# Gate tiles of the merge moved to the start, in pairs by seven half products, and one merge stage at the end

## The chip, the cores and the metric

The kernel runs on one core of a Trainium2 chip. The metric is the device time of one execution in microseconds (us), as the median of three runs; one further execution was profiled. TensorE (PE in the rows) multiplies, VectorE (DVE), ScalarE (ACT) and GpSimd (POOL) do the elementwise work, and SyncE (SP) issues the transfers.

## The reference

One layer of an encoder for 1024 prompt tokens and 64 sample tokens that share the weights, all in fp32. Four token mixers (A: mLSTM, B: forgetting attention, C: HGRN2, D: convolution and RG-LRU) read columns of one projection of x and give y_m with 512 columns. Each is expanded to 1024 columns and gated by a product of x, and the four are summed:

```python
proj = jnp.einsum('btd,dp->btp', x, w_in) + b_in          # split among the mixers A, B, C, D
...
for m_idx, y_b in enumerate((y_ml, y_fx, y_hg, y_rg)):
    gate = jax.nn.sigmoid(jnp.einsum('btd,de->bte', x, w_mg[m_idx]) + b_mg[m_idx])
    terms.append(gate * jnp.einsum('btw,wd->btd', y_b, w_br[m_idx]))
mix = terms[0] + terms[1] + terms[2] + terms[3]
x1 = layer_norm(DN_ALPHA * x + jnp.einsum('btd,de->bte', mix, w_out), ln1_g, ln1_b)
gate_pre = jnp.einsum('btd,df->btf', x1, w_ff_gate)
up = jnp.einsum('btd,df->btf', x1, w_ff_up)
...
ffn = jnp.einsum('btf,fd->btd', jax.nn.gelu(gate_c) * up, w_ff_down)
x2 = layer_norm(DN_ALPHA * x1 + ffn, ln2_g, ln2_b)
```

The outputs are x2 for both groups and the mixers' states. Only the order and the arithmetic of the gates and of the sum over mixers are touched by the change.

## The kernel before

Activations stand transposed: 128 channels on the partitions, 1088 tokens in three chunks of 384, 384 and 320 columns. Each fp32 operand is split into a high and a low part, and every product is three matmuls (high by high, high by low, low by high; `mm3`, lines 296 to 298). A **dense tile** (`dense`) is 128 output channels of a product of x: for each chunk 8 k-blocks by 3 matmuls into a PSUM buffer of the pool "psd", then one eviction. The pools "psd" and "psm" have two buffers each.

Weights come in the order of a list, `plan`; a tile of 512 KB is loaded by SP two places ahead (`wissue`), its high part converted by POOL (projections, line 259) or ACT (all others, line 261) and its low part by DVE (line 262).

The mixers run in the order D, C, B, A, in units: P_x(u) is the projections of unit u and M_x(u) its recurrence or attention, made of many small matmuls and elementwise operations. `weave` sends the steps of M_x(u-1) and of P_x(u) by turns. The last M of a branch is woven with 12 chunk steps of **gate tiles** (`gates`: a dense tile of x by w_mg, and a tanh on ACT, line 682, into `th`). Then `merge(m, it)` follows: it computes the other four gate tiles, loads y of the branch (`yr`), splits it (lines 701, 702), multiplies by w_br into "psm" (12 matmuls a chunk), and DVE gates the product (line 717: (th + 1) times the product). The sum over branches goes through DRAM: from the second branch on `prev` is loaded from mx_d and added (line 719), and the first three branches store `th` to mx_d.

After the last merge come w_out and the first LayerNorm (F), the FFN's gate and up products (G), and the down projection (H). In G two tiles of 128 outputs are computed together by `pair` (products at line 368): the first two token chunks and the two halves of k form a 2 by 2 block product with seven block products instead of eight, on sums of weight blocks (`wsums`, lines 284 and 285 for the split) and of x blocks (`xsums`); the third chunk is computed plainly. One block product is 12 matmuls of 384 columns.

At the start the nine tiles of x are transposed by PE and split (lines 177 to 189), the projections' biases are transposed, the first tile of P_D(0) runs between these, and `gate_rows` computes 48 small rows (the scalar gates of A and B) from w16r, a gather of 16 columns of w_in (lines 540 to 549).

Of the kernel before, what the change touches and what calls it, by code (L numbers as in the profile page):

```python
# [2 lines left out]

# [16 lines left out]
P = 128  # L20
# [9 lines left out]
NSLOT = 19  # L30
TGRP = ((0, 1, 2), (3, 4, 5), (8, 6, 7))
# [37 lines left out]
def trunk_kernel(ctx: ExitStack, tc: tile.TileContext, I, O, dbg=None):  # L69
# [36 lines left out]
    slot_pool(NSLOT)  # L106
# [33 lines left out]
    maskU = const([P, P], "maskU")  # L140
# [4 lines left out]
    trif = slot([P, P], F32, "trif")  # L145
# [20 lines left out]
    def xtiles(s):  # L166
        for c, (n0, n) in enumerate(CH):
# [32 lines left out]
    def plan_cons(m):  # L200
        for kind, e in (("mg", 0), ("mg", 1), ("mg", 2), ("mg", 3), ("mg", 4), ("mg", 5), ("br", 0), ("br", 2),
                        ("mg", 6), ("mg", 7), ("br", 4), ("br", 6)):
            wide = P if kind == "mg" else 2 * P
            plan.append(((kind, m, e), I["w_" + kind][0, m, :, e * P:e * P + wide].rearrange(
                "(k p) c -> p k c", p=P), 1024 // wide))

    for u in range(4):
        for c0 in (RG_X, RG_G):
            plan.append((("in", c0 + u * P), win(c0 + u * P), 8))
    plan_cons(3)  # L210
    for u in range(4):
# [17 lines left out]
    pairs = {}  # L229
# [92 lines left out]
    def xsums():  # L322


        for j in (0, 1, 3):
            xs[j] = tuple(wide["x"].tile([P, 4, 384], F32R, tag=f"x{j}{i}", name=nm("xs"), bufs=1) for i in range(2))
        xs[2] = tuple(t[1][:, 0:4, :] for t in (xh, xl))
# [12 lines left out]
        for k in range(4):  # L340
            b11, b12, b22 = temp("xf", 0, k), temp("xf", 1, k), temp("xf", 1, k + 4)
            t3.append(temp("x3"))
            V.tensor_tensor(b11, b12, b11, OP.subtract)
            V.tensor_tensor(t3[k], b22, b12, OP.subtract)
            V.tensor_tensor(b22, b22, b11, OP.subtract)
            parts(0, k, b11)
            parts(1, k, b22)
        for k in range(4):
# [3 lines left out]
            parts(2, k, t3[k])  # L352
# [79 lines left out]
    pkr = slot([P, P], F32, "pkr")  # L432
    pk2 = const([P, PK2], "pk2")
    pk2r = slot([P, P], F32, "pk2r")
    xt = {}

    def xload(*tts):
        for tt in tts:
            xt[tt] = slot([P, D], F32, "xt")
# [1343 lines left out]
```

## Time and profile before

| what | value |
|---|---|
| median of three runs | 2143.22 us (2140.59 to 2143.59) |
| the profiled execution | 2141.45 us |
| its span, first to last instruction | 2139.7 us |
| mean granted clock of TensorE | 0.998 |
| PE busy | 2101.1 us, 98% of the span |
| DVE busy | 1151.5 us, 54% |
| ACT busy | 737.1 us, 34% |
| POOL busy | 223.7 us, 10% |

The engines work side by side; a share is that of the whole span, and stages with different limits lie in it. Matmuls are pipelined, so the time printed beside one is longer than the distance from its start to the next one's.

### The profile page before, as it was taken

The numbers are of one execution on the slowest core, as the hardware profiler recorded it, in microseconds if no ns is written. First come the engines' busy times: TensorE is split into PE (matmuls) and PEld (weight loads), VectorE is DVE, ScalarE is ACT, GpSimd is POOL, SyncE is SP. The second block draws the span as 40 slices with busy tenths as digits, with TensorE's granted clock in tenths as the row PEclk, the third lists the DMA queues.
The fourth block names the chain that finished last, engine by engine and source line by source line (L and its number), as shares of the span: only waits on it lengthen the run. The fifth ranks groups of instructions, "written<-read, shape, count | busy, mean of one in ns | idle before, by whom it ended". The sixth has DMA issues, their size and how long they took to land.

```text
span 2139.7 us, 31840 instructions
## 1 busy us (share of the span) xinstructions
PE 2101.1 (98%) x13035; PEld 1955.5 (91%) x13035; DVE 1151.5 (54%) x2202; ACT 737.1 (34%) x1277; POOL 223.7 (10%) x232
## 2 busy tenths in 40 slices
PE   8999999999999999999999999999999999999998
PEld 7999999888899988889999989899889999998886
DVE  4643245665543466555332144546459766666655
ACT  3664114555321234344310123324134333334341
POOL 1100011220100322200001101000120000000112
PEclk9999999999999999999999999999999999999999
DMA  5112321111143222321432212135211222227652
GB/s 153 53 61 71 103 75 40 44 45 33 52 148 132 82 81 61 92 82 41 131 136 82 63 38 65 43 123 194 80 74 51 80 88 74 79 87 282 224 198 100
DMA packets 193229, 200.29 MB, mean 94 GB/s; under 512 B 14588, under 2 KB 165448, under 8 KB 193084
## 3 DMA queue, kind: packets, MB, share of 16 engines
q1 hardware_dynamic: 193084, 198.26, 28.8%
q8 instruction: 102, 1.67, 0.3%
q14 instruction: 43, 0.35, 0.1%
HBM read 154.80 MB, written 43.43 MB: 93 GB/s over the span
## 4 chain that ended last, share of the span: by engine, by line
PE 51%; DVE 2%; DMA 1%; ACT 0%; issue 0%; POOL 0%; SPq 0%; DVEq 0%; ACTq 0%
PE pss L368 8%; PE psd L296 7%; PE psd L298 7%; PE psd L297 7%; PE pss L1693 5%; PE psd L1693 2%; PE psm L1693 2%; PE psm L297 2%; PE psm L296 2%; PE psm L298 2%; PE pss L296 1%; PE pss L297 1%; PE pss L298 1%; PE psm L368 1%; PE psm L1330 1%; PE psm L1117 0%
## 5 line engine op out<-in xcount | busy, mean ns | idle before, releaser
L296 PE MATMUL psd<-xh,wh 128*128 128x384 f32 (+1 forms) x1920 | 643.2, 335 | 0.9 <-ACT xh L178 0.9
L298 PE MATMUL psd<-xh,wl 128*128 128x384 f32 (+1 forms) x1920 | 631.4, 329 | 0.0
L297 PE MATMUL psd<-xl,wh 128*128 128x384 f32 (+1 forms) x1920 | 630.1, 328 | 0.8 <-DVE xl L179 0.8
L262 DVE TENSOR_TENSOR wl<-wr,wh 128x1024 fp32r<-128x1024 f32 x179 | 222.7, 1248 | 327.6 <-ACT wh L261 202.5
L296 PEld LDWEIGHTS psd<-xh,wh 128*128 128x128 f32 x1920 | 362.9, 189 | 7.9 <-issue 3.0
L297 PEld LDWEIGHTS psd<-xl,wh 128*128 128x128 f32 x1920 | 361.6, 188 | 1.8 <-DVE xl L179 1.0
L298 PEld LDWEIGHTS psd<-xh,wl 128*128 128x128 f32 x1920 | 361.6, 188 | 0.4
L261 ACT ACTIVATE wh<-wr 128x1024 fp32r<-128x1024 f32 x131 | 139.0, 1061 | 376.6 <-PE psd L297 127.5
L297 PE MATMUL psm<-yl,wh 128*128 128x384 f32 (+1 forms) x384 | 125.9, 328 | 1.4 <-DVE yl L702 1.4
L298 PE MATMUL psm<-yh,wl 128*128 128x384 f32 (+1 forms) x384 | 125.7, 327 | 0.0
L296 PE MATMUL psm<-yh,wh 128*128 128x384 f32 (+1 forms) x384 | 125.0, 328 | 0.6 <-ACT yh L701 0.6
L259 POOL TENSOR_SCALAR wh<-wr 128x1024 fp32r<-128x1024 f32 x48 | 52.7, 1098 | 669.7 <-PE psd L297 266.5
L682 ACT ACTIVATE th<-psd,bhalf 128x384 f32<-128x384 f32 (+1 forms) x96 | 53.4, 558 | 156.0 <-PE psd L298 156.0
L717 DVE SCALAR_TENSOR_TENSOR th<-th,psm 128x384 f32<-128x384 f32 (+1 forms) x96 | 50.9, 531 | 104.5 <-PE psm L298 103.2
L296 PE MATMUL psd<-x1h,wh 128*128 128x320 f32 (+1 forms) x272 | 85.2, 313 | 0.6 <-DVE x1l L189 0.6
L298 PE MATMUL psd<-x1h,wl 128*128 128x320 f32 (+1 forms) x272 | 84.9, 312 | 0.0
L297 PE MATMUL psd<-x1l,wh 128*128 128x320 f32 (+1 forms) x272 | 84.7, 312 | 0.0
L1496 POOL TENSOR_TENSOR lrs<-lrs,mhalf 128x1 f32<-128x1 f32 (+1 forms) x16 | 9.8, 614 | 665.9 <-ACT hh L1640 423.9
L1180 DVE CUSTOM_DVE_ANT_0 Pt<-pss,fcb 128x128 f32<-128x128 f32 (+7 forms) x64 | 48.2, 752 | 57.6 <-PE pss L1175 57.1
L297 PEld LDWEIGHTS psm<-yl,wh 128*128 128x128 f32 x384 | 72.1, 188 | 2.1 <-DVE yl L702 2.1
L296 PEld LDWEIGHTS psm<-yh,wh 128*128 128x128 f32 x384 | 71.8, 188 | 1.5 <-ACT yh L701 1.2
L298 PEld LDWEIGHTS psm<-yh,wl 128*128 128x128 f32 x384 | 72.1, 188 | 0.0
(536 smaller groups left out, 3907.4 us busy)
## 6 DMA issues: line engine op xcount, KB each, us to landing
wr<-in_w_in_dram SPq DMA_DIRECT2D x48, 512.0 KB
wr<-in_w_ff_down_dram SPq DMA_DIRECT2D x48, 512.0 KB
wr<-in_w_mg_dram SPq DMA_DIRECT2D x32, 512.0 KB
mx_d<-th SPq DMA_DIRECT2D x24, 544.0 KB
prev<-mx_d SPq DMA_DIRECT2D x24, 544.0 KB
wr<-in_w_br_dram SPq DMA_DIRECT2D x16, 512.0 KB
wr<-in_w_ff_gate_dram SPq DMA_DIRECT2D x16, 512.0 KB
wr<-in_w_ff_up_dram SPq DMA_DIRECT2D x16, 512.0 KB
```

The costliest lines, as they stand in the source:

```text
L259: G.tensor_scalar(h, raw, 1.0, 1.0, OP.mult, OP.mult)
L261: S.activation(h, raw, AF.Copy)
L262: V.tensor_sub(l, raw, h.bitcast(F32))
L296: PE.matmul(ps, wh, mh, start=i == 0, stop=False)
L297: PE.matmul(ps, wh, ml, start=False, stop=False)
L298: PE.matmul(ps, wl, mh, start=False, stop=i == n - 1)
L368: PE.matmul(ps, w[:, k, :], x[:, k, :], start=start and k == 0 and i == 0, stop=k == 3 and i == 2, skip_group_check=not start)
L682: S.activation(th[:, n0:n0 + n], ps, AF.Tanh, bias=b, scale=0.5)
L717: V.scalar_tensor_tensor(th[:, n0:n0 + n], th[:, n0:n0 + n], 1.0, ps[:, :n], OP.add, OP.mult)
L1180: V.tensor_tensor_reduce(Pt[:, 0:L].rearrange("p (b n) -> p b n", b=nb), ps.rearrange("p (b n) -> p b n", b=2)[:, 0:nb, 0:n], cbs[hh][:, 0 ...
L1330: PE.matmul(ps[0:w, 0:w], kt[r, t0:t0 + w], qt[r, t0:t0 + w], start=True, stop=True)
L1693: PE.matmul(ps[hf], a[:, f % 8, o:o + P], w[:, 0, sl], start=f == 0 and i == 0, stop=f == 15 and i == (2 if tt < 8 else 1))
```

## The change

The 32 gate tiles no longer depend on where the mixers are, since they need x alone. Thirty of them now come first: four of branch 3 plainly while x is still being transposed, then 13 pairs through `pair`, with the sums of x made by `xsums(False)` into tiles of their own. Every `th` is stored to DRAM (`th_d`), 544 KB each. The last two, (0,6) and (0,7), run plainly under M_A(1). The mixers follow one another without a merge: the last M of a branch is woven with the next branch's projections, M_C(3) with 7 of the steps of P_B(0), and M_A(1) with 14 steps, of which six are the last two gate tiles and eight are merge pieces (one chunk of one output tile) of branch 3. Then all other merges follow. y is loaded from y_d and split into the tiles of x, which x no longer needs (`ysplit`), `th` is loaded from th_d, and the sum over branches stays in eight tiles on chip (`res`), chunk by chunk. The load order `plan` follows. At the start the first weights are gate tiles, so ACT converts them, and the gates' biases (pk2r) are loaded ahead of the projections' biases (pkb).

In numbers of instructions: PE has 11475 instead of 11631 rows, DVE 2377 instead of 2142, ACT 75 more, and SP issues 32 stores and 32 loads of `th` where it issued 24 stores and 24 loads of the running sum.


```diff
+PLAIN = ((3, 0), (3, 2), (0, 6))
...
+    th_d = [[dp.tile([P, T], F32, name=f"th_d{m}_{e}") for e in range(8)] for m in range(4)]
+
+    def gates(m, es):
+        for e in es:
+            th = slot([P, T], F32, "th")
+            b = bhalf[:, m * 8 + e:m * 8 + e + 1]
+
+            def ev(c, n0, n, ps, th=th, b=b):
+                S.activation(th[:, n0:n0 + n], ps, AF.Tanh, bias=b, scale=0.5)
+                if c == 2:
+                    SP.dma_start(th_d[m][e], th)
+            yield from dense(("mg", m, e), ev)
+
+    def gate_pair(m, e):
+        ths = [slot([P, T], F32, "th") for _ in range(2)]
+        bs = [bhalf[:, m * 8 + e + i:m * 8 + e + i + 1] for i in range(2)]
+
+        def act(i, n0, n, src):
+            S.activation(ths[i][:, n0:n0 + n], src, AF.Tanh, bias=bs[i], scale=0.5)
+
+        def add(i, n0, ps, other):
+            V.tensor_tensor(ths[i][:, n0:n0 + 384], ps, other, OP.add)
+            if n0 == 384:
+                a = 384 * i
+                act(i, a, 768 - a, ths[i][:, a:768])
+                if i == 0:
+                    SP.dma_start(th_d[m][e], ths[0])
+
+        def put(i, n0, n, ps):
+            act(i, n0, n, ps)
+            if i == 1 and n0 == 0:
+                SP.dma_start(th_d[m][e + 1], ths[1])
+        yield from pair(("mg", m, e), ("mg", m, e + 1), add, put)
+
+    g0, g1 = gates(3, (0,)), gates(3, (1,))
+    for c in range(3):
+        for tt in range(3 * c, 3 * c + 3):
+            if c:
+                xsplit(xt[tt], tt, tt != 3 * c + 1)
+        next(g0)
+        next(g1)
+    run(g0, g1, gates(3, (2, 3)))
+    xsums(False)
...
+    def ysplit(m, c):
+
+        n0, n = CH[c]
+        for q in range(0, 4, 2):
+            r = slot([P, 2, 384], s="yr")
+            for i in range(2):
+                SP.dma_start(r[:, i, 0:n], y_d[m][q + i][:, n0:n0 + n])
+            k = 4 * (m % 2) + q
+            h = xh[c][:, k:k + 2, :]
+            S.activation(h, r[:, :, 0:n], AF.Copy)
+            V.tensor_sub(xl[c][:, k:k + 2, :], r[:, :, 0:n], h.bitcast(F32))
...
+    def merge(m, es, rows=None):
+
+        for e in es:
             wh, wl = wget(("br", m, e))
             for g in range(2):
...
+                th = slot([P, T], F32, "th")
+                SP.dma_start(th, th_d[m][e + g])
+                if m == 3:
+                    res.append(th)
                 for c, (n0, n) in enumerate(CH):
...
+                    ps = bank("m")[:, :n]
+                    y = [[t[c][:, 4 * (m % 2) + k, :] for k in range(4)] for t in (xh, xl)] if rows is None else \
+                        [[t[k][:, n0:n0 + n] for k in range(4)] for t in rows]
+                    mm3(ps, [(wh[:, k, g * P:(g + 1) * P], wl[:, k, g * P:(g + 1) * P], y[0][k], y[1][k])
+                             for k in range(4)])
+                    sl = slice(n0, n0 + n)
+                    V.scalar_tensor_tensor(th[:, sl], th[:, sl], 1.0, ps, OP.add, OP.mult)
+                    if m < 3:
+                        V.tensor_tensor(res[e + g][:, sl], res[e + g][:, sl], th[:, sl], OP.add)
+                    yield
...
-    def branch(m, Pg, Mg, n, nP, nM, it, ng=4):
-        for u in range(1, n):
-            weave(Mg(u - 1), nM, Pg(u), nP)
-        weave(Mg(n - 1), nM, gates(m, range(4)), 12)
-
-    first = P_D(0)
-    for c in range(1, 3):
-        next(first)
-        for tt in range(3 * c, 3 * c + 3):
-            xsplit(xt[tt], tt, tt != 3 * c + 1)
-        next(first)
-    next(first)
+    def until_flushed(g):
+
+        while tails:
+            next(g)
+            flush()
+        run(g)
+
+    for m, e in mgs:
+        if (m, e) not in PLAIN:
+            run(gate_pair(m, e))
+    slot_pool(NSLOT)
+    phase("D")
     gate_rows()
-    run(first)
-    branch(3, P_D, M_D, 4, 6, 10, 0)
-    merge(3, 0)
+    run(P_D(0))
+    weave(M_D(0), 10, P_D(1), 6)
+    weave(chain(M_D(1), fox_rows()), 13, P_D(2), 6)
+    weave(M_D(2), 10, P_D(3), 6)
+    weave(chain(M_D(3), ml_rows()), 17, P_C(0), 12)
     out_D()
     phase("C")
-    weave(chain(fox_rows(), ml_rows()), 10, P_C(0), 12)
-    branch(2, P_C, M_C, 4, 12, 19, 1)
-    merge(2, 1)
+    for u in range(1, 4):
+        weave(M_C(u - 1), 19, P_C(u), 12)
+    g = P_B(0)
+    weave(M_C(3), 19, islice(g, 7), 7)
+    until_flushed(g)
     phase("B")
-    run(P_B(0))
-    branch(1, P_B, M_B, 4, 9, 23, 2)
-    merge(1, 2)
+    for u in range(1, 4):
+        weave(M_B(u - 1), 23, P_B(u), 9)
+    weave(M_B(3), 23, P_A(0), 18)
     phase("A")
-    run(P_A(0))
-    branch(0, P_A, M_A, 2, 18, 21, 3)
-    res = merge(0, 3)
+    weave(M_A(0), 21, P_A(1), 18)
+
+    def last_gates():
+        for i, _ in enumerate(gates(0, (6, 7))):
+            if i >= 3:
+                xtiles("y", (i - 3,))
+                ysplit(3, i - 3)
+            yield
+
+    g = chain(last_gates(), merge(3, (0, 2)))
+    weave(M_A(1), 21, islice(g, 14), 14)
+    until_flushed(g)
+    for c in range(3):
+        ysplit(2, c)
+    run(merge(3, (4, 6)))
+    for c in range(3):
+        ysplit(1, c)
+    run(merge(2, (0, 2, 4, 6)))
+    rows = yrows()
+    run(merge(1, (0, 2, 4, 6)), merge(0, (0, 2, 4, 6), rows))
```

Where instructions now stand (order of issue on one engine; the names are tiles of the program with running numbers, written `out<-in`).

SP's queue, before, in the start: the load of w16r behind two loads of projection weights.

```order
L251 DMA wr_312<-in_w_in_dram 128x8x128
L251 DMA wr_380<-in_w_in_dram 128x8x128
L540 DMA w16r_527<-in_w_in_dram 128x8x8
L541 DMA w16r_527<-in_w_in_dram 128x8x8
L543 DMA b_55_530<-in_b_in_dram 8x1
```

SP's queue, after, where the pairs end and branch D begins; th_2847 to th_3029 are gates of the last two pairs.

```order
L516 DMA th_d_2_228<-th_2847 128x1088
L263 DMA wr_3331<-in_w_in_dram 128x8x128
L521 DMA th_d_5_231<-th_3029 128x1088
L263 DMA wr_3503<-in_w_in_dram 128x8x128
L516 DMA th_d_4_230<-th_3028 128x1088
L601 DMA w16r_3205<-in_w_in_dram 128x8x8
L602 DMA w16r_3205<-in_w_in_dram 128x8x8
L604 DMA b_374_3208<-in_b_in_dram 8x1
```

w16r now stands behind the stores of the gates; on PE, 37 matmuls of the first projections stand between the last product of the last pair and the 48-row products that read it.

PE, before, where M_C(3) begins: 24 matmuls into psd_5072 stand between the first and the second of these rows of transposes.

```order
L957 MATMUL psm_5059<-ident,vT_4538 128x128 x4
L296 MATMUL psd_5072<-xh_118,wh_4738 128x384
...
L957 MATMUL psm_5098<-ident,vT_4538 128x128 x4
L957 MATMUL psm_5104<-ident,vT_4538 64x128
L296 MATMUL psd_5107<-xh_120,wh_4738 128x384
...
L957 MATMUL psm_5133<-ident,kU_5055 128x128 x4
```

PE, after, at the same place (xh is a chunk of x, wh_6494 a projection weight of branch B): 13 matmuls into psd stand between the second and the last group of v transposes.

```order
L1012 MATMUL psm_6789<-ident,vT_6294 128x128 x4
L1012 MATMUL psm_6795<-ident,vT_6294 128x128 x4
L310 MATMUL psd_6801<-xh_131,wl_6298 128x320
L308 MATMUL psd_6857<-xh_127,wh_6494 128x384
...
L1012 MATMUL psm_6827<-ident,vT_6294 64x128
L308 MATMUL psd_6857<-xh_127,wh_6494 128x384
...
L1012 MATMUL psm_6830<-ident,kU_6785 128x128 x4
L1012 MATMUL psm_6836<-ident,kU_6785 128x128 x4
```

The transposes and what follows from them stand closer together.

DVE, before, in M_A(1): a step of the unit, with the low part of one weight (L262) among its operations.

```order
L1340 TENSOR_SCALAR kp_12617<-psm_12612,aw_12348 128x64
L1339 TENSOR_TENSOR we_12622<-we_12622,psm_12615 128x128
L262 TENSOR_TENSOR wl_12694<-wr_12691,wh_12693 128x1024
L1363 TENSOR_TENSOR mnum_12339<-mit_12659,pss_12652 128x129
L1370 SCALAR_TENSOR_TENSOR mC_2007_12662<-mC_1990_12566,mbc,pss_12652 64x129
```

DVE, after, in M_A(1): L782 gates a merge piece (psm_12400, psm_12440), L747 is the low part of two y rows.

```order
L1418 TENSOR_TENSOR mnum_11909<-mit_12421,pss_12414 128x129
L1449 TENSOR_SCALAR mnum_11921<-mnum_11921,bmv_1953_11922,vr_12376 128x128 x4
L1425 SCALAR_TENSOR_TENSOR mC_2063_12424<-mC_2045_12344,mbc,pss_12414 64x129
L782 SCALAR_TENSOR_TENSOR th_12290<-th_12290,psm_12400 128x320
L1433 BN_STATS bst_12426<-mnum_11909 128x6
...
L1425 SCALAR_TENSOR_TENSOR mC_2066_12433<-mC_2050_12367,mbc,pss_12415 64x129
L1433 BN_STATS bst_12435<-mnum_11921 128x6
L747 TENSOR_TENSOR yl_12088<-yr_12815,yh_12087 128x768
L1434 BN_AGGR bmv_1953_11922<-bst_12435 128x2
L782 SCALAR_TENSOR_TENSOR th_12438<-th_12438,psm_12440 128x384
```

DVE, which before only served the unit and the weights here, now also empties the merge pieces, which share "psm" with the unit's scores, and splits y.

## Rows read from the trace of the kernel before

**Rows 1.** The page: busy time of each engine, and GB/s in 40 slices.
```profile
PE 2101.1 (98%) x13035; PEld 1955.5 (91%) x13035; DVE 1151.5 (54%) x2202; ACT 737.1 (34%) x1277; POOL 223.7 (10%) x232
...
GB/s 153 53 61 71 103 75 40 44 45 33 52 148 132 82 81 61 92 82 41 131 136 82 63 38 65 43 123 194 80 74 51 80 88 74 79 87 282 224 198 100
```

**Rows 2.** The page: chain that ended last, share of the span by engine.
```profile
PE 51%; DVE 2%; DMA 1%; ACT 0%; issue 0%; POOL 0%; SPq 0%; DVEq 0%; ACTq 0%
```

**Rows 3.** PE's waits: line waited for, us in total, times, longest us.
```profile
PE psm L957 <- DVE vt L961: 8.3, 4, 3.3
PE pss L177 <- DMA xt<-in_x_prompt_dram: 4.6, 1, 4.6
```

**Rows 4.** Timeline of PE in a merge: start us, us, line, operation, tiles, shape.
```profile
1471.37 0.30 PE L296 MATMUL psm<-yh,wh 128*128 128x320 f32 x1
...
1473.12 0.34 PE L296 MATMUL psm<-yh,wh 128*128 128x384 f32 x1
...
1477.30 0.30 PE L296 MATMUL psm<-yh,wh 128*128 128x320 f32 x1
```

**Rows 5.** Chain of waits in the FFN stage: start us, us, what.
```profile
1713.93 6.35 PE pss L368 x36
...
1823.60 6.52 PE pss L368 x36
```

**Rows 6.** Groups: instructions, busy us, mean ns of one, idle before.
```profile
L262 DVE TENSOR_TENSOR wl<-wr,wh 128x1024 fp32r<-128x1024 f32 x179 | 222.7, 1248 | 327.6 <-ACT wh L261 202.5 <-POOL wh L259 106.1 <-PE psm L1089 10.6
...
L717 DVE SCALAR_TENSOR_TENSOR th<-th,psm 128x384 f32<-128x384 f32 (+1 forms) x96 | 50.9, 531 | 104.5 <-PE psm L298 103.2 <-PE psm L839 1.2
...
L702 DVE TENSOR_TENSOR yl<-yr,yh 128x1088 fp32r<-128x1088 f32 x12 | 15.7, 1312 | 24.5 <-ACT yh L701 24.5
...
L378 ACT ACTIVATE pp<-pss 128x384 f32<-128x384 f32 x42 | 20.3, 484 | 41.8 <-PE pss L368 38.4 <-DVE gp L1591 3.3
```

**Rows 7.** Windows: busy us of PE, PEld, DVE, ACT, POOL; clock, DMA, GB/s; a group.
```profile
1616.00:1935.00 319.00, 318.92 (x1921) 313.29 (x1920) 235.67 (x408) 112.67 (x167) 0.00 (x0) 1.00 0.27 80
1060.00:1140.00 80.00, 80.00 (x487) 79.91 (x486) 29.90 (x38) 9.74 (x15) 2.63 (x3) 1.00 0.43 151
1295.00:1375.00 80.00, 80.00 (x506) 71.70 (x504) 41.92 (x183) 27.10 (x70) 10.43 (x10) 1.00 0.20 64
...
L1409 DVE SCALAR_TENSOR_TENSOR mso<-mso,zn 128x512 f32<-128x512 f32 (+1 forms) x8 | 4.5, 557 | 0.0
```

**Rows 8.** The start: timeline of PE, SP's queue and DVE, and one window.
```profile
15.50 0.52 PE L296 MATMUL psd<-xh,wh 128*128 128x384 f32 x1
15.82 0.52 PE L297 MATMUL psd<-xl,wh 128*128 128x384 f32 x1
...
21.46 1.13 SPq L540 DMA_DIRECT2D w16r<-in_w_in_dram  x1
...
32.34 0.22 DVE L549 CAST w<-w16r 128x128 fp32r<-128x128 f32 x1
...
14.00:19.00 5.00, 5.00 (x21) 5.00 (x21) 0.84 (x1) 0.00 (x0) 0.00 (x0) 0.66 0.49 138
```

**Rows 9.** Branch C's last unit: timeline of PE, POOL and DVE, and one window.
```profile
540.62 0.65 PE L957 MATMUL psm<-ident,vT 128*128 128x128 f32 x4
...
549.20 0.30 PE L957 MATMUL psm<-ident,vT 128*64 128x128 f32 x1 [3.32 <-DVE vt L961]
...
562.29 0.65 PE L989 MATMUL psm<-KX,qc 128*32 128x128 f32 x16
...
545.91 2.08 POOL L949 TENSOR_TENSOR kU<-z,eU 128x1088 f32<-128x1088 f32 x1
...
564.72 0.29 DVE L1013 COPY ot<-pss 128x128 f32<-128x128 f32 x1 [0.24 <-PE pss L1012]
...
567.04 0.29 DVE L1013 COPY ot<-pss 128x128 f32<-128x128 f32 x1 [0.84 <-PE pss L1012]
...
549.20:552.60 3.40, 3.40 (x20) 3.40 (x21) 1.33 (x3) 0.00 (x0) 0.00 (x0) 1.00 0.00 0
```

More of the change, by code (lines that the diff above doesn't have):

```diff
@@ L2 @@
 from contextlib import ExitStack
+from itertools import islice
 import concourse.bass as bass
@@ L98, in slot_pool @@
         slots[0] = ExitStack()
+        uid[0] += 1
         for name in beside:
-            wide[name] = slots[0].enter_context(tc.tile_pool(name=f"{name}{n}", bufs=2, reuse_waits="tile"))
-        slots[1] = slots[0].enter_context(tc.tile_pool(name=f"tp{n}", bufs=n, reuse_waits="tile"))
+            wide[name] = slots[0].enter_context(tc.tile_pool(name=f"{name}{uid[0]}", bufs=2, reuse_waits="tile"))
+        slots[1] = slots[0].enter_context(tc.tile_pool(name=f"tp{uid[0]}", bufs=n, reuse_waits="tile"))
         temps[0] = None
@@ L164, in trunk_kernel, with xtiles @@
     xh, xl = {}, {}
-    def xtiles(s):
-        for c, (n0, n) in enumerate(CH):
+    def xtiles(s, chunks=(0, 1, 2)):
+        for c in chunks:
+            n = CH[c][1]
             xh[c] = xp_.tile([P, 8, n], F32R, tag=f"xh{c}", name=nm(s + "h"))
@@ L320, in trunk_kernel, with xsums @@
     xs = {}
[L322 to L327, printed above, removed]
+    def xsums(over):
+        for j in range(4):
+            if j == 2 and over:
+                xs[j] = tuple(t[1][:, 0:4, :] for t in (xh, xl))
+            else:
+                xs[j] = tuple(wide["x"].tile([P, 4, 384], F32R, tag=f"x{2 * j + i}", name=nm("xs"), bufs=1)
+                              for i in range(2))
         def temp(tag, c=None, k=None):
@@ L341, in xsums @@
             b11, b12, b22 = temp("xf", 0, k), temp("xf", 1, k), temp("xf", 1, k + 4)
-            t3.append(temp("x3"))
             V.tensor_tensor(b11, b12, b11, OP.subtract)
+            t3.append(temp("x3") if over else b12)
             V.tensor_tensor(t3[k], b22, b12, OP.subtract)
@@ L347, in xsums @@
             parts(1, k, b22)
+            if not over:
+                parts(2, k, b12)
         for k in range(4):
@@ L351, in xsums @@
             V.tensor_tensor(b21, b21, t2, OP.subtract)
-            parts(2, k, t3[k])
+            if over:
+                parts(2, k, t3[k])
             parts(3, k, b21)
@@ L438, in xload @@
         for tt in tts:
-            xt[tt] = slot([P, D], F32, "xt")
+            xt[tt] = wide["x"].tile([P, D], F32, tag=f"x{tt}", name=nm("xt"), bufs=1) if tt < 8 else slot([P, D], F32, "xt")
             pinned(SP.dma_start(xt[tt][0:tw(tt)], xsrc(tt)))
@@ L535, in trunk_kernel @@
     me_d = dp.tile([8, 9], F32, name="me_d")
-    mx_d = [[dp.tile([P, T], F32, name=f"mx_d{i}_{e}") for e in range(8)] for i in range(3)]
     def gate_rows():
@@ L656, in ml_rows @@
             yield
-    y_d = [[dp.tile([P, T], F32, name=f"y_d{m}_{j}") for j in range(3)] for m in range(4)]
+    y_d = [[dp.tile([P, T], F32, name=f"y_d{m}_{j}") for j in range(4 if m else 3)] for m in range(4)]
     ylast = {}
@@ L674, in yput, with yrows @@
             ylast[m] = y
-    def gates(m, es):
-        for e in es:
-            th = slot([P, T], F32, "th")
-            b = bhalf[:, m * 8 + e:m * 8 + e + 1]
-            def ev(c, n0, n, ps, th=th, b=b):
-                S.activation(th[:, n0:n0 + n], ps, AF.Tanh, bias=b, scale=0.5)
-            ths[m, e] = th
-            yield from dense(("mg", m, e), ev)
-    def merge(m, it):
-        res = []
+    res = []
+    def ysplit(m, c):
[8 more added lines that the diff above has]
+            V.tensor_sub(xl[c][:, k:k + 2, :], r[:, :, 0:n], h.bitcast(F32))
+    def yrows():
         yh, yl = [], []
-        g4 = gates(m, (4, 5))
-        while tails:
-            next(g4)
-            flush()
         for j in range(4):
@@ L1058, in P_B @@
             V.tensor_sub(kk[q], k32[r], kk[r].bitcast(F32))
-        ks = small([P, TS], "fks", 2)
+        ks = cp.tile([P, TS], F32, tag="fks", name=nm("fks"), bufs=2)
         G.tensor_copy(ks, k32[:, TP:T])
```

105 lines of the change are left out of this document (45 added, 60 removed).

## The prediction

> **What bounds the kernel now.** I read the page's busy times first. TensorE (PE) is busy 2101.1 us of a span of 2139.7, VectorE (DVE) for 54% of it, and no fortieth of the span moves more than 282 GB/s [rows 1]. Half of the chain of work that ended last is PE, against 2% for DVE and 1% for DMA [rows 2]; what the chain doesn't put into these few per cent is matmul following matmul. The list of PE's waits is short: the largest is 8.3 us for four waits of one transpose, the next the 4.6 us before the first input lands [rows 3]. So PE's own work is the time. A change pays what it takes off PE's instruction list, less what it adds to PE's waits. DVE, ACT or DMA work counts only where PE has nothing else to do.
>
> The price of one matmul is not the 0.33 us printed beside it, since they overlap, but the distance from start to start. In a dense stretch 24 products of 384 columns begin between 1473.12 and 1477.30, which is 174.2 ns each, and 12 of 320 columns between 1471.37 and 1473.12, 146 ns each [rows 4].
>
> **The saving.** PE's list shrinks from 11631 to 11475 rows: 13 pairs of gate tiles each lose one of eight half products on their first 768 tokens, 12 matmuls of 384 columns, 156 in all. Nothing else leaves or enters PE. At 174.2 ns this is 27.2 us. A second way: the FFN stage already runs such pairs, and there the same block of 36 products starts at 1713.93 and, five pairs on, at 1823.60 [rows 5], so a pair takes 21.93 us. Two plain tiles are 96 x 0.1742 + 48 x 0.146 = 23.73 us, so a pair saves 1.80 us and 13 pairs 23.4. I take 25, with 23.4 and 27.2 as ends.
>
> **Work added off PE.** The pairs add weight sums: 26 rounds of an ACT conversion and a DVE subtraction as wide as those of a weight (1.25 us on DVE), their sums, and 39 copies of 0.48 us [rows 6]; the merge adds 384-wide sums in place of 24 sums of a whole row. These lie under PE. In the FFN stage, which has the same pairs and a convolution as well, DVE is busy 235.67 of 319 us and PE 318.92 [rows 7]. Without that cover the sums would cost some 3 us a pair. The merge stage at the end has 32 th tiles of 544 KB, 16 weights of 512 KB and 16 y rows, 35 MB over 32 x 5.93 = 190 us of PE: 185 GB/s, where a merge of before ran at 151 GB/s with PE full [rows 7] and the down projection at 282 [rows 1]. DVE there needs some 1.0 us for each 12 products of 2.09 us. I cost both at nothing; a queue that falls behind is a rival below. The 24 stores and 24 loads of the running mix go away and 32 and 32 of the gates come, also nothing.
>
> **The start.** Before, PE waits 4.6 us for the first rows of x [rows 3], and some of the first products then stand 0.32 us apart [rows 8], the half clock (1.2 GHz) after a halting beginning: granted clock 0.66 in that stretch of 5 us. After, the same waits for x and for the first split remain; ACT converts the first weights, queued with the split of x, and two gate tiles instead of one mixer tile are ready between the transposes. Bounds -2 (the slow stretch goes) to +3 (it comes twice). I take +0.5.
>
> **From the pairs to branch D.** Now 48 small products for the recurrent gates wait for w16r, whose load SP issues only behind the store of the last pair's gates (the order of instructions, first place). The store waits for the last tanh, some 2.2 us behind the last product (copy 0.48 [rows 6], a sum of about the same, and a tanh of twice the width). Before, the first of its two issues stands at 21.46 and takes 1.13 us, and its first reader runs at 32.34 [rows 8]: so 2.3 us at least (two issues) and 10.9 at most from issue to use. I take 6 (an estimate between the ends, a little to the lower, since DVE had other work ahead of that reader), with 0.7 for the casts: 8.9 us. Behind the last product PE still has 37 dense ones, 6.4 us. Stall 2.5, taken as 3; bounds 0 and 7. Queued behind it are branch D's first matmuls and so everything. [...]
>
> **Branch C's last unit.** It was woven with 12 chunks of gates, and now has 7 steps of branch B's projections. In the trace of before, the v transposes start at 540.62 and the last waits until 549.20 for DVE, 3.32 us of it idle, although 24 dense products lay between; the k transposes' input leaves POOL at 545.91 + 2.08 = 547.99, and scores start at 562.29 [rows 9]. Now 13 dense products lie there, and 8 transposes (order, second place): 8.58 - 2 x 0.65 - 13 x 0.174 = 5.0 us idle, 1.7 more than before. After that, scores can start some 9 us sooner than before, and the nine steps then run close to their own chain, one state copy from the next 2.32 us [rows 9]; six of the steps hold 55 dense products (9 us) and some 50 small ones (about 5), against 13.9 us of chain. I add 2. Together +4; bounds 0 and 9.
>
> **Branch A's last unit.** This is the dearest place. Its 12 dense steps become 6 dense ones and 8 merge pieces of 12 products. Dense tiles use another PSUM pool and ACT empties them; a merge piece uses the two buffers that the unit's own scores use, and DVE empties it, behind the unit's operations (order, third place). From the first merge piece to the ninth, PE has 108 products (6 x 12 x 0.174 + 3 x 12 x 0.146 = 17.8 us) and 59 small ones, at most 0.174 each: 28 us. DVE's list for that stretch: 9 evictions at 0.531 (4.8), 7 half rows of y subtracted, at a 768 or 640 wide share of 1.31 us (6.0) [rows 6], 2 weight remainders at 1.25 (2.5), 3 of 0.557 (1.7), and some 130 small operations. In the window of before DVE was busy 41.92 us over 183 operations [rows 7]; less 4 remainders (5.0) and 8 outputs (4.5) that is 0.19 each, 24.7. Sum 39.7 against 28. Neighbouring stretches are lighter on DVE, and PE can run ahead by two buffers, but not by 11 us. I take +7; bounds 0 (DVE's overlap hides it) and +15. Late next would be the unit's scores, then all merges.
>
> **The sum.** -25 + 0.5 + 3 + 4 + 7 = -10.5. The profiled execution took 2141.45 (1.75 outside its span), so 2131; the median of the runs shown, 2143.22, is 1.8 above it, so 2132.7. I predict 2132.
>
> **Rivals.** 1. All waits hide: PE keeps its 98%, and the time is 2143.2 - 27.2 or less the start's 2, so 2115 to 2118. For it: before, PE is busy 80.00 of 80 us in the window of branch A's last unit [rows 7]. Against: ACT emptied the dense tiles there.
> 2. The waits eat the gain: M_A at +15, C at +9, the transition at +7 and the start at +0.5 against -25 give +6.5; with two of the three at their ends it is 2139 to 2144, no change. For it: the y loads of the merge sit in SP's queue behind the store of gate tile (0,6) and in slots that the unit still holds.
> 3. Slower: PE's clock falls in branch A's last unit. The waits there come every step. If the granted clock falls to half for the stretch, its 28 us of PE work take 28 more, as the 0.32 against 0.174 us in the start [rows 4, 8] show, and the sum becomes +17: 2160. It decides from about 10 us of it at half clock beside the other terms. Against: behind the 3.32 us wait of branch C the clock stays at 1.00 [rows 9]. The Trainium skill (TensorE: Matmul & The Clock Gate, section HAM oscillation) has this as a known failure, groups of matmuls parted by waits that each start at the low clock; the start of this trace agrees with it (0.66), branch C does not.
> 4. The transfers of the merge fall behind: a th or y load late by one 544 KB transfer at 185 GB/s is 3 us; ten of the 32 late would give back 30 and end near 2160 too. Nothing in the rows of before shows PE waiting for a load there.
>
> **How the numbers follow.** What this kernel can show as a change is about 0.2%, 4.3 us; faster is below 2138.9, slower above 2147.5. Chances: my case with its own range of 2122 to 2139, 0.54; rival 1, 0.22; rival 2, 0.14; rival 3, 0.03; rival 4, 0.07. Range: 2115 at rival 1's end; upwards to 2145, which takes in most of rival 2 and leaves out 3 and half of 4. Faster: 0.22 from rival 1, 0.52 from mine, 0.04 from rival 2, 0.78. Same: 0.02 from mine, 0.08 from rival 2, 0.03 from rival 4, 0.13. Slower: 0.02 from rival 2, 0.03 from rival 3, 0.04 from rival 4, 0.09.
>
> **What would show it.** PE's matmul count down by 156 and a pair cadence near 21.9 us in the first 400 us. A wait of PE on DVE's w cast of about 3 us where branch D begins. The wait on the copy of vt at branch C's last unit longer than 3.3 us. Waits of PE on psm, released by DVE, between the first merge pieces, 7 us together. No PE wait on th or yr loads, granted clock near 1.00 throughout. Wrong would be: a wait of over 10 us on a load in the merge stage, a clock below 0.9 in any stretch behind the start, or no waits at all in branch A's last unit, which is rival 1.

## The result, and the profile after

The changed kernel takes 2154.55 us (median of four runs, 2151.54 to 2157.02) against 2142.88 for the kernel before (also four runs): 1.0056 times the time before, with an interval of 1.0038 to 1.0073. It is slower by 0.56%, and lies outside the range that was forecast.

The page of the changed kernel, busy times; its span is 2153.9 us and its mean granted clock 0.991:

```profile
PE 2095.9 (97%) x12879; PEld 1939.7 (90%) x12879; DVE 1283.2 (60%) x2438; ACT 791.9 (37%) x1352; POOL 223.9 (10%) x232
```

Beside [rows 1] PE has 156 instructions fewer and is busy only 5.2 us less, where 27 less were worked out; and it idles 58.0 us of its span where it idled 38.6. Two things have grown: the waits, by 19.4 us, and the time of the matmuls themselves, since the mean granted clock went from 0.998 to 0.991. The two mean clocks make some 30 us more at half clock (1.2 instead of 2.4 GHz), which costs at most 15 us of matmul time, an estimate from these figures and the spans. Where the waits are, from the changed kernel's list of PE's waits (us in total, times, longest):

```profile
PE psm L1012 <- DVE vt L1016: 8.3, 5, 3.1
PE pss L181 <- DMA xt<-in_x_prompt_dram: 4.7, 1, 4.7
PE psm L644 <- DMA clf<-in_cache_fox_logf_dram: 4.3, 1, 4.3
...
PE psm L308 <- DVE we L1394: 2.7, 4, 1.2
PE psd L308 <- ACT xh L182: 2.6, 2, 1.7
...
PE psm L308 <- DVE th L782: 2.3, 2, 1.9
PE psm L714 <- DVE mli L684: 2.2, 1, 2.2
PE psm L1459 <- DVE mnum L1449: 2.2, 1, 2.2
PE psm L308 <- ACT zn L1463: 1.9, 3, 0.8
...
PE psm L308 <- DVE xp L811: 1.2, 1, 1.2
```

The first two answer to [rows 3] and are as long as they were. New are the wait for clf (the cached forget gates that `fox_rows` transposes), the one for xp right behind it, the one for mli (`ml_rows`), and a family on psm in branch A's last unit (L308 in the merge, L1459). Where the clock fell, from windows of the changed kernel (busy us of PE, PEld, DVE, ACT, POOL, then granted clock, DMA share, GB/s):

```profile
100.00:440.00 340.00, 338.72 (x2030) 330.16 (x2029) 149.58 (x201) 135.09 (x195) 13.42 (x11) 1.00 0.29 91
455.00:460.45 5.45, 1.16 (x10) 0.73 (x9) 3.62 (x1) 0.00 (x0) 1.47 (x1) 1.00 0.38 108
460.45:470.70 10.25, 8.67 (x35) 7.26 (x34) 2.80 (x6) 7.47 (x11) 0.00 (x0) 0.50 0.10 10
525.00:545.00 20.00, 17.76 (x110) 16.46 (x109) 12.53 (x31) 10.84 (x13) 1.57 (x2) 0.91 0.12 31
745.00:765.00 20.00, 16.15 (x91) 14.08 (x90) 17.82 (x27) 6.23 (x14) 11.12 (x8) 0.83 0.18 59
780.00:1240.00 460.00, 452.24 (x3278) 401.33 (x3277) 238.46 (x620) 159.43 (x376) 84.50 (x121) 1.00 0.24 69
1265.00:1325.00 60.00, 52.46 (x313) 44.78 (x313) 46.91 (x174) 23.26 (x54) 5.82 (x6) 0.94 0.70 184
1325.00:1365.00 40.00, 38.12 (x221) 37.64 (x220) 22.52 (x36) 10.10 (x11) 0.00 (x0) 0.96 0.57 199
```

The pairs themselves are clean: 1.3 us idle and full clock from 100 to 440. The wait for clf itself still shows a clock of 1.00 (455 to 460.45), and the 10.25 us behind it run at half. The other windows with long waits, at 525, 745, 1265 and 1325, have a clock below 1. Not all waiting does this: from 780 to 1240 PE idles 7.8 us, in waits of 1.2 us and less, at full clock. The 156 matmuls were saved in the first row, and paid back in the rows whose clock is below 1 and in the waits.

### The profile page after: what moved, and what is told of

Read it like the earlier page. It is cut to its first block, busy times and chain, and to the rows that moved or that the text cites. A ratio compares the mean times of both kernels' runs of the same rounds, so it can differ in the third digit from the quotient of the medians.

```text
span 2153.9 us, 32071 instructions
## 1 busy us (share of the span) xinstructions
PE 2095.9 (97%) x12879; PEld 1939.7 (90%) x12879; DVE 1283.2 (60%) x2438; ACT 791.9 (37%) x1352; POOL 223.9 (10%) x232
## 4 chain that ended last, share of the span: by engine, by line
PE 46%; DVE 3%; DMA 1%; issue 0%; POOL 0%; ACT 0%; DVEq 0%; SPq 0%; ACTq 0%; POOLq 0%
PE pss L386 8%; PE pss L1769 5%; PE psd L308 4%; PE psd L310 4%; PE psd L309 4%; PE psm L308 3%; PE psm L310 3%; PE psm L309 3%; PE psd L1769 2%; PE psm L1769 2%; PE pss L308 1%; PE pss L310 1%; PE pss L309 1%; PE psm L386 1%; PE psm L1385 1%; PE psm L1172 0%
## 5 line engine op out<-in xcount | busy, mean ns | idle before, releaser
L308 PE MATMUL psd<-xh,wh 128*128 128x384 f32 (+1 forms) x1504 | 504.7, 336 | 3.0 <-ACT xh L182 2.6
L310 PE MATMUL psd<-xh,wl 128*128 128x384 f32 (+1 forms) x1504 | 494.2, 329 | 0.0
L309 PE MATMUL psd<-xl,wh 128*128 128x384 f32 (+1 forms) x1504 | 493.5, 328 | 0.4 <-DVE xl L183 0.4
L308 PEld LDWEIGHTS psd<-xh,wh 128*128 128x128 f32 x1504 | 286.4, 190 | 9.9 <-issue 3.4
L309 PEld LDWEIGHTS psd<-xl,wh 128*128 128x128 f32 x1504 | 285.0, 189 | 1.9 <-DVE xl L183 0.9
L310 PEld LDWEIGHTS psd<-xh,wl 128*128 128x128 f32 x1504 | 285.0, 189 | 0.4
L386 PE MATMUL pss<-xs,sh 128*128 128x384 f32 x536 | 136.9, 336 | 0.0
L308 PE MATMUL psm<-yh,wh 128*128 128x384 f32 (+1 forms) x384 | 128.6, 335 | 6.9 <-DVE we L1394 2.7
L297 DVE TENSOR_TENSOR sl<-st,sh 128x1024 fp32r<-128x1024 f32 x54 | 66.1, 1224 | 51.9 <-ACT sh L296 51.5
L386 PEld LDWEIGHTS pss<-xs,sh 128*128 128x128 f32 x536 | 96.1, 188 | 0.1
L386 PE MATMUL pss<-xs,sl 128*128 128x384 f32 x268 | 90.0, 336 | 0.0
L308 PE MATMUL psd<-x1h,wh 128*128 128x320 f32 (+1 forms) x272 | 85.3, 313 | 0.6 <-DVE x1l L193 0.6
```

Source lines behind the costliest of these rows:

```text
L297: V.tensor_sub(l, t, h.bitcast(F32))
L308: PE.matmul(ps, wh, mh, start=i == 0, stop=False)
L309: PE.matmul(ps, wh, ml, start=False, stop=False)
L310: PE.matmul(ps, wl, mh, start=False, stop=i == n - 1)
L386: PE.matmul(ps, w[:, k, :], x[:, k, :], start=start and k == 0 and i == 0, stop=k == 3 and i == 2, skip_group_check=not start)
```

## The experiments

All ratios are to the kernel before, timed beside each, with 95% intervals; 0.1% is 2.1 us. The kernels ran on more than one chip, so two of them are compared by their ratios first.

| kernel | median us | ratio | interval |
|---|---|---|---|
| changed | 2154.55 | 1.0056 | 1.0038 to 1.0073 |
| e1_plain | 2174.77 | 1.0135 | 1.0120 to 1.0151 |
| e2_clf_early | 2153.35 | 1.0042 | 1.0027 to 1.0057 |
| e3_merge_psd | 2152.54 | 1.0035 | 1.0022 to 1.0049 |
| e4_ma_gates | 2159.84 | 1.0065 | 1.0050 to 1.0080 |
| e5_fill | 2161.46 | 1.0077 | 1.0061 to 1.0093 |
| e6_rows | 2150.74 | 1.0032 | 1.0022 to 1.0042 |
| e7_rows_psd_yr | 2145.24 | 1.0005 | 0.9992 to 1.0017 |
| e8_held | 2136.51 | 0.9976 | 0.9967 to 0.9986 |
| e9_mlB | 2137.71 | 0.9979 | 0.9970 to 0.9988 |
| e10_before_rows | 2156.93 | 1.0068 | 1.0054 to 1.0081 |

**Do the pairs save anything?** e1_plain computes the same tiles in the same place without pairs.

```diff
-            run(gate_pair(m, e))
+            run(gates(m, (e, e + 1)))
```

> The changed kernel with its 13 pairs computed as 26 plain tiles (8 half products a pair again, no weight sums); all else as changed. Theory (the pairs save what their cadence says, and the loss lies elsewhere): the stretch of the gate tiles takes 13 x (23.73 - 22.06) = 21.7 us longer, the time is about 2154.5 + 21.7 = 2176, and the waits behind it stay. Rival (the pairs bring nothing, the first stage itself is slow): the time stays within 5 us of 2154.

It took 20.2 us more than the changed kernel by the medians, 17 by the ratios, and the waits behind the stretch stayed. The product that waits for clf starts at 480.24 us instead of 459.82, 20.4 us later. The theory holds: the pairs pay nearly what their cadence says. The loss, some 30 us, lies elsewhere.

**Is the wait for clf a late load?** e2_clf_early issues it where branch D begins.

```diff
     gate_rows()
+    clf = small([P, 8, 8], "clf", 1)
+    SP.dma_start(clf, I["cache_fox_logf"][0, 0].rearrange("(t p) h -> p t h", p=P))
     run(P_D(0))
```

> The changed kernel with the load of clf (the cached log forget gates) issued where branch D begins, instead of behind the store of a branch D output. Theory (PE's 4.3 us wait for clf is late issue, and the 10.2 us at half clock behind it are its consequence): no wait on clf, no half clock at 460 us, 7 to 10 us less, about 2146. Rival A (the clock falls there anyway, since the place is thin in matmuls): 4 us less, about 2150, half clock stays. Rival B (the next link of the same chain is late instead): under 2 us less.

Some 3 us less by the ratios, 1.2 by the medians, with intervals that overlap; the time does not tell the theory from rival B, the trace does. The timeline of this kernel, DVE and PE at the same place:

```profile
453.65 4.18 DVE L636 TENSOR_TENSOR_SCAN cr<-fx 8x1024 f32<-8x1024 f32 x1 [0.35 <-DMA fx<-ls_d]
...
457.76 2.25 DVE L646 TENSOR_TENSOR_SCAN cc<-cl 8x1024 f32<-8x1024 f32 x1
...
460.39 0.15 DVE L810 COPY xp<-pk 128x3 f32<-128x3 f32 x1
...
460.59 0.66 PE L308 MATMUL psm<-uh,wabh 128*128 128x384 f32 x1 [3.77 <-DVE xp L810]
461.05 0.52 PE L309 MATMUL psm<-ul,wabh 128*128 128x384 f32 x1
461.37 0.52 PE L310 MATMUL psm<-uh,wabl 128*128 128x384 f32 x1
```

The load's wait of 4.3 us is gone, and the wait for xp, one link on, is 3.8 us instead of 1.2: two scans of eight rows hold DVE for 6.4 us, the next unit's first operation (a copy of 0.15 us) is queued behind them, and PE has no dense work left to fill the time. The products behind it again stand 0.32 us apart (461.05 to 461.37). That is rival B.

**Which part of branch A's last unit waits?** e3_merge_psd gives the merge pieces the other PSUM pool; e4_ma_gates puts four plain gate tiles there and all merge pieces behind the unit.

```diff
-                    ps = bank("m")[:, :n]
+                    ps = bank("d")[:, :n]
```

> The changed kernel with the merge pieces multiplied into the PSUM pool psd instead of psm. Theory (in branch A's last unit the merge pieces wait for buffers that the unit's own scores hold, and that DVE empties in order): the waits of PE on psm in merge pieces between 1265 and 1325 us fall from about 5 us to under 2, with at least one of the three half clock pieces gone: 4 to 9 us less, 2146 to 2150. Rival (DVE's list is simply too long there, 39.7 us of operations against 28 of matmuls): the waits move to other rows and the time stays within 2 us of 2154.

```diff
-PLAIN = ((3, 0), (3, 2), (0, 6))
+PLAIN = ((3, 0), (3, 2), (0, 4), (0, 6))
...
-    weave(M_A(1), 21, islice(g, 14), 14)
+    weave(M_A(1), 21, islice(g, 12), 12)
```

> The changed kernel with four plain gate tiles (12 chunks, 0/4 to 0/7) under branch A's last unit as before, and every merge piece behind it; one pair fewer. Theory (merge pieces are the wrong cover there): the 7 us of waits inside the unit and two half clock pieces (3.4 us) go, the pair costs 1.7 back: about 8 us less, 2146. Rival (the waits follow the merge pieces to wherever they begin, because y is loaded and split late): under 3 us less.

The same window in e3_merge_psd, then the two parts of it in e4_ma_gates:

```profile
1265.00:1325.00 60.00, 57.46 (x359) 49.04 (x359) 49.94 (x187) 25.77 (x58) 5.11 (x6) 1.00 0.72 198
```

```profile
1240.00:1295.00 55.00, 54.22 (x354) 47.93 (x353) 34.12 (x136) 23.37 (x54) 4.93 (x4) 1.00 0.45 139
1295.00:1315.00 20.00, 11.19 (x44) 9.85 (x43) 10.86 (x37) 5.37 (x10) 1.09 (x2) 0.74 0.89 200
```

With buffers of its own, PE idles 2.5 us there instead of 7.5 and the clock stays at 1.00, though DVE is as full as before: in this window sharing psm made most of the waits, not the length of DVE's list. One wait of 2.1 us, at the unit's last output, stays. The whole time is 4.5 us less by the ratios, the low end of what the theory gave, and 2.0 by the medians, which is the rival's figure; the intervals overlap, so the window decides and the time does not.

With e4's cover the unit itself runs full, but behind it PE works 11.2 of 20 us at a clock of 0.74. Two waits make most of the idle time: 3.8 us for the unit's last output, and 4.1 us for a merge piece, behind rows of y that land late:

```profile
1300.06 0.36 PE L1460 MATMUL psm<-ident,mnum 64*128 64x64 f32 x1 [3.82 <-DVE mnum L1450]
...
1307.11 0.84 ACT L747 ACTIVATE yh<-yr 128x768 fp32r<-128x768 f32 x1 [6.33 <-DMA yr<-y_d]
1307.98 0.96 DVE L748 TENSOR_TENSOR yl<-yr,yh 128x768 fp32r<-128x768 f32 x1 [6.19 <-ACT yh L747]
1308.86 0.48 DVE L783 SCALAR_TENSOR_TENSOR th<-th,psm 128x320 f32<-128x320 f32 x1
...
1309.40 0.69 PE L309 MATMUL psm<-yh,wh 128*128 128x384 f32 x1 [4.14 <-DVE th L783]
```

On DVE the operation that empties PE's buffer (L783) stands behind the split of y (L748), which idles 6.2 us until the load is there. My theory that the pieces are the wrong cover fell, and the rival of the expectation came true in part: the waits followed the merge pieces, because y is loaded and split late. The other part is the end of the unit, which has no dense work beside it.

**Can idle products hold the clock?** e5_fill puts unread products ahead of three waits (54 matmuls more to do).

```diff
+        fill(24)
         for g in range(2):
             pt = bank("m")
...
         V.memset(mcol, 0.0)
+        fill(12)
...
+                if u == 3 and g0 == 8 and not eng:
+                    fill(18)
```

> The changed kernel with idle products put in front of three waits, whose result nobody reads: 24 products of x by itself (4.2 us) ahead of the transposes of clf, 12 ahead of those of mli, 18 ahead of the last v transposes of branch C's last unit. PE has 54 matmuls (9.4 us) more to do. Theory (half of what was lost is the clock that falls behind a wait): the fill takes the place of the waits of 4.3, 2.2 and 3.1 us, the clock stays at 1.00 at 460, 532 and 757 us, and 20.5 us at half clock become full: 7 to 10 us less, about 2146. Rival (the clock costs nothing since PE waits there anyway): within 2 us of 2154. Rival 2 (the waits are dependencies that only move): up to 9 us more.

Slower by 4.5 us by the ratios, 6.9 by the medians; PE still waits 3.0 us for clf, and the clock still falls at 459 us. But the trace shows that the edit did not put the fill where the question needs it:

```profile
442.75 4.32 PE L635 MATMUL psd<-xh 128*128 128x384 f32 x24
...
455.81 0.38 SPq L263 DMA_DIRECT2D wr<-in_w_in_dram  x1
456.24 0.58 SPq L643 DMA_DIRECT2D clf<-in_cache_fox_logf_dram  x1
...
460.23 1.87 PE L650 MATMUL psm<-ident,clf 128*8 128x128 f32 x8 [3.03 <-DMA clf<-in_cache_fox_logf_dram]
```

The 24 products run 10 us ahead of the wait, with dense products between. The load of clf is issued 0.65 us earlier than in the changed kernel (456.24 against 456.89), so the fill did not hold it up; its reader starts 0.4 us later all the same (460.23 against 459.82). A load of weights (wr) stands right in front of it here, which may be why; no run shows it. So this kernel doesn't separate the price of the clock from that of the waits, and that is left open.

**Are the rows in the wrong place?** e6_rows weaves them with the second half of P_C(0); e7_rows_psd_yr adds e3's edit and splits the last rows of y later, behind half of branch 1's merge.

```diff
-    weave(chain(M_D(1), fox_rows()), 13, P_D(2), 6)
+    weave(M_D(1), 10, P_D(2), 6)
...
-    weave(chain(M_D(3), ml_rows()), 17, P_C(0), 12)
+    g = P_C(0)
+    weave(M_D(3), 10, islice(g, 6), 6)
     out_D()
+    weave(chain(fox_rows(), ml_rows()), 10, g, 6)
```

> The changed kernel with the row work of branches B and A (fox_rows, ml_rows) taken out of the chains behind M_D(1) and M_D(3) and woven with the second half of P_C(0), as before it was woven with all of P_C(0); M_D(3) gets the first half. Theory (the row scans stand on DVE ahead of the next unit's first operations, 4.18 and 2.25 us each, and PE has nothing to do then; woven with projections that ACT empties they cost nothing): no waits over 1 us between 400 and 545 us, no half clock there: 6.5 us of waits and half of 13.6 us at half clock, 10 to 13 us less, about 2142. Rival (six dense chunks are too thin for both): under 4 us less, with the waits at mli again.

> The rows of branches B and A woven with the second half of P_C(0), the merge pieces in the PSUM pool psd, and the split of branch 0's rows of y moved behind the first half of merge(1). Theory (the waits add up, and their clock): against the changed kernel 11 us less for the rows, 4 to 5 for psd (as its run alone showed), 2 for y, 17 less in all: 2137, faster than before by 6 us. Rival (each repair only moves the idle time to the next join, since dense work is gone from the joins): 2146 to 2150.

By the ratios 5 us less and 11 less than the changed kernel, where 10 to 13 and 17 were expected. PE's waits of e7_rows_psd_yr between 500 and 570 us show what is left:

```profile
PE psm L1012 <- DVE vt L1016: 3.7, 2, 2.7
PE psm L644 <- DMA clf<-in_cache_fox_logf_dram: 2.6, 1, 2.6
PE psd L308 <- ACT gs L922: 1.2, 1, 1.2
PE psm L894 <- DVE stD L887: 0.9, 1, 0.9
```

Six dense chunks for M_D(3) and six for the rows are half of what each had before, and the waits add up to 8.4 us. I took dense chunks to be what was missing, and two kernels bring some. Both keep e7's other two edits (the merge pieces in psd, the later split of y), and their diffs are shown against e7_rows_psd_yr. e8_held holds one pair back as plain tiles for M_D(3), so that the rows stand under all of P_C(0) again; e9_mlB sends ml_rows on to branch B, giving up no pair.

```diff
-    g = P_C(0)
-    weave(M_D(3), 10, islice(g, 6), 6)
+    weave(M_D(3), 10, gates(0, (4, 5)), 6)
     out_D()
-    weave(chain(fox_rows(), ml_rows()), 10, g, 6)
+    weave(chain(fox_rows(), ml_rows()), 10, P_C(0), 12)
```

> The kernel with rows, psd and y repaired, and one pair of gate tiles (0/4 and 0/5) held back as two plain tiles, six dense chunks woven with M_D(3), so that all 12 chunks of P_C(0) lie under the row work as before. Theory (what the change took away is dense work that waits for nothing but x, at the places where chains are long): the pair costs 1.7 us back, and the waits between 505 and 565 us (7.5 us in that kernel) and the half clock behind them (10 us, 5 lost) fall by more than half: 2145.2 + 1.7 - 8 = 2139, faster than before by 3 to 6 us. Rival (the idle time moves on to the next join): 2145 to 2147.

```diff
-    weave(M_D(3), 10, islice(g, 6), 6)
+    weave(M_D(3), 10, islice(g, 7), 7)
     out_D()
-    weave(chain(fox_rows(), ml_rows()), 10, g, 6)
+    weave(fox_rows(), 3, g, 5)
...
+    weave(chain(M_B(0), ml_rows()), 30, P_B(1), 9)
```

> The kernel with rows, psd and y repaired, and the rows of branch A (ml_rows) moved on behind M_B(0), woven with P_B(1); M_D(3) gets seven chunks of P_C(0) and fox_rows five. No pair is given up. Theory (enough dense work for each chain): the waits between 505 and 565 us fall by half, branch B hides the other rows: about 2141. Rival (DVE's scans then stand before branch B's own operations): 2145 or more.

Both are faster than the kernel before, by 0.24% and 0.21%, and by some 17 us than the changed kernel; some 11 of these are e7's. e8_held does it with one pair fewer. PE's waits in the same stretch, first in e8_held from 478 to 570 us, then in e9_mlB from 500 to 570:

```profile
PE psm L1013 <- DVE vt L1017: 3.4, 1, 3.4
PE psm L645 <- DMA clf<-in_cache_fox_logf_dram: 2.1, 1, 2.1
PE psm L895 <- DVE stD L888: 1.1, 1, 1.1
```

```profile
PE psm L1012 <- DVE vt L1016: 1.9, 1, 1.9
PE psm L894 <- DVE stD L887: 0.9, 1, 0.9
PE psd L308 <- ACT gs L922: 0.2, 1, 0.2
```

In e9_mlB they fell from 8.4 us to 3.0, as expected. In e8_held they fell only to 6.6, where less than half was expected, so the 6 us that it gained on e7_rows_psd_yr are not these waits alone; where the rest lies was not followed up. The page of e9_mlB, whose span is 2136.2 us at a mean clock of 0.996:

```profile
PE 2089.6 (98%) x12879; PEld 1933.3 (91%) x12879; DVE 1280.1 (60%) x2438; ACT 786.3 (37%) x1349; POOL 220.0 (10%) x232
```

**The part alone.** e10_before_rows does to the kernel before only what the change did to the rows.

```diff
-    branch(3, P_D, M_D, 4, 6, 10, 0)
+    weave(M_D(0), 10, P_D(1), 6)
+    weave(chain(M_D(1), fox_rows()), 13, P_D(2), 6)
+    weave(M_D(2), 10, P_D(3), 6)
+    weave(chain(M_D(3), ml_rows()), 17, gates(3, range(4)), 12)
     merge(3, 0)
...
-    weave(chain(fox_rows(), ml_rows()), 10, P_C(0), 12)
+    run(P_C(0))
```

> The kernel before, with one part of the change alone: fox_rows behind M_D(1), woven with P_D(2), and ml_rows behind M_D(3), woven with the 12 gate chunks that stood there; P_C(0) by itself. Merges and gate tiles as before. Theory (the placing of the rows, not the pairs, made these waits): a wait of 3 to 5 us at clf and half clock behind it where M_D(1) ends, nothing at ml_rows since gate chunks cover it: 6 to 10 us more, about 2151. Rival (they only cost where the gates are gone): within 2 us of 2143.

It is 0.68% slower, some 14.6 us, more than the 6 to 10 that the theory gave. Its page:

```profile
PE 2107.5 (98%) x13035; PEld 1960.0 (91%) x13035; DVE 1158.0 (54%) x2202; ACT 737.1 (34%) x1278; POOL 223.0 (10%) x232
```

The longest of PE's waits that is new, and the window from the middle of it on:

```profile
PE psm L583 <- DMA clf<-in_cache_fox_logf_dram: 4.8, 1, 4.8
```

```profile
118.06:131.70 13.64, 9.88 (x39) 8.06 (x40) 5.08 (x7) 7.47 (x11) 0.00 (x0) 0.50 0.19 28
```

The span is 2155.8, 16.1 more than in the profile before: with the same 13035 matmuls PE is busy 6.4 us longer (clock 0.994 against 0.998) and idle 9.7 us longer. The join with clf takes most of it: PE idles 6.5 us there (4.8 for clf, 1.3 for xp, 0.4 behind it), and 9.9 us of its work run at half clock. The join with mli, which has its 12 gate chunks here, costs 1.6 us of waits. One part is at a place that the edit did not touch, the wait for vt in branch C's last unit:

```profile
562.69 0.42 PE L957 MATMUL psm<-ident,vT 128*64 128x128 f32 x1 [3.28 <-DVE vt L961]
```

```profile
561.80:568.60 6.80, 5.91 (x19) 5.91 (x20) 2.23 (x5) 0.00 (x0) 0.00 (x0) 0.50 0.00 0
```

It is as long as the 3.32 us of [rows 9], and behind it the same dense products run at half clock here and at full clock there. That is some 3 us of the 14.6 (half of 5.91, an estimate), which may be chance and not the price of the rows. So the join with clf alone cost some 11 us (6.5 and half of 9.9, an estimate), about half of what the pairs save.

## Why the prediction was wrong

**Pairs, -25:** right, a little high. In the changed kernel one product of a pair's block in psm, and the same product nine pairs on, start at

```profile
117.22 0.33 PE L386 MATMUL psm<-xh,wh 128*128 128x384 f32 x1
...
315.79 0.33 PE L386 MATMUL psm<-xh,wh 128*128 128x384 f32 x1
```

which is 22.06 us a pair against the 21.93 of [rows 5]; that makes 21.7 us for 13, and e1_plain gave 17 to 20.

**Start, +0.5:** the waits there are about 1.5 us longer (xh and L190 among them), and the slow stretch did not go. Dense products stand 0.32 us apart from 16.82 to 20.02 us, where before they did so from 15.18 to 18.38:

```profile
17.14 0.52 PE L308 MATMUL psd<-xh,wh 128*128 128x384 f32 x1
17.46 0.52 PE L309 MATMUL psd<-xl,wh 128*128 128x384 f32 x1
```

It was not tried further.

**From the pairs to branch D, +3:** PE waited 0.3 us. w16r's first issue is at 364.46 and its cast at 368.48, so 4 us and not 6, and the 37 dense products covered nearly all of it.

**Branch C's last unit, +4:** the wait for vt is 3.1 us, as long as before; the 1.7 and 2 I added did not come. What came is a clock of 0.83 in the 20 us around it, of which the sum knew nothing.

**Branch A's last unit, +7:** PE idles 7.5 us in the window from 1265, most of it by the mechanism named (e3_merge_psd shows it), and 1.9 in the next. The term was nearly right for the waits; the clock of 0.94 and 0.96 there comes on top and had no term.

**The step that failed** is one that has no term. The sum went through the joins that lost gate tiles or merges, and passed over the lines `chain(M_D(1), fox_rows())` and `chain(M_D(3), ml_rows())`: the row work that stood under 12 dense chunks was taken as moved at no cost. The runs showed in its place a cost of the size of the whole slowdown. The changed kernel has its longest new wait there, 4.3 us for clf, then 1.2 for xp and 2.2 for mli, and some 12 us of PE's work at half clock behind them (8.67 in the window at 460; about 3.5 in the one at 525, by its clock of 0.91), half of which is lost: 7.7 + 6, some 14 us, an estimate from these rows. e10_before_rows, the same part alone, is 14.6 us slower than the kernel before, some 3 of them elsewhere. e6_rows gave back only 5, since waits of 4.7 us (for clf, gs and stD, the same as in e7_rows_psd_yr) stand at the place where it puts the rows.

**The second failure** is rival 3 and its chance of 0.03. I let the clock fall in one place only, and took one wait of 3.32 us at full clock behind it [rows 9] as proof that such waits are harmless. In the changed kernel the same wait, 3.1 us, has a lower clock behind it, and in e10_before_rows a wait of 3.28 us at the same place has. So have the waits at 455 and 525 in the changed kernel, and the clock is below 1 in branch A's last unit. The rule that I cited from the Trainium skill (TensorE: Matmul & The Clock Gate, section HAM oscillation), that groups of matmuls parted by waits start at the low clock, was the better guide: the windows at 455 to 470 and e10_before_rows agree with it, the one wait of before does not. What the lower clock costs can be read from busy time at equal work, 6.4 us in e10_before_rows. When a wait of some 3 us brings the fall and when not, no run shows.

Rival 2, the waits eat the gain, is nearest to what happened; its place was wrong, and its price too low, because each wait was counted once, and not with the slow products behind it. That the end of the kernel would not suffer from transfers (rival 4) held in the changed kernel, but for one late row of y: 1.9 us at 1360; in e4_ma_gates late rows cost 4.1. Rival 1's own figures give 2114 to 2116 and not 2115 to 2118; nothing hangs on it.

## What to carry to other kernels

When work that depends on nothing but the input is moved away from where it stands, price the places that it leaves, and not only the place where it goes: it was the filler for every chain that had to wait for another engine. Walk every line of the new order for a chain whose dense partner got shorter, the short preparatory ones too, and count a wait together with the slow matmuls that may follow it. The plain change lost all of the pairs' 21.7 us and more. With the merge pieces in buffers of their own, a later split of y and either some dense work held back (e8_held) or a chain sent on to a place that has cover (e9_mlB), about a quarter was kept: 5.1 and 4.5 us. No run has the last step without the other two.

## What was not expected of the hardware

The clock stood at half behind waits of 2.2 to 4.8 us in kernels whose PE is busy 97 and 98% of the span, and the same wait for vt had it behind it in two kernels (3.14 and 3.28 us) and not in another (3.32 us). The runs of one kernel differ with it: the changed kernel's four runs read 2151.54, 2153.49, 2155.62 and 2157.02 us at mean clocks of 0.993, 0.992, 0.991 and 0.989.

The scan of 8 rows by 1024 took 2.28 us in e10_before_rows, where POOL was idle beside it. It took 3.96 us in the changed kernel and 4.18 in e2_clf_early, where POOL was multiplying a full tile when it began, and in both it ended 2.1 to 2.2 us behind POOL's product. In the changed kernel:

```profile
452.86 3.61 POOL L888 TENSOR_TENSOR gg<-h,gg 128x1088 f32<-128x1088 f32 x1 [3.85 <-DVE h L886]
...
454.66 3.96 DVE L636 TENSOR_TENSOR_SCAN cr<-fx 8x1024 f32<-8x1024 f32 x1 [0.55 <-DMA fx<-ls_d]
```

So the scan got little done while POOL's product ran: an inference from these times, which no run was made to test.
